# Inverse norms to row form: nine spreads on TensorE replaced by two transfers through DRAM each

## The chip, the cores and the metric

The kernel runs on one core of a Trainium2 chip. The metric is the device time of one execution in microseconds (us). Engines are named as in the profile: PE is TensorE, DVE is VectorE, ACT is ScalarE, POOL is GpSimd, SP is SyncE, which here only issues transfers.

## The reference, cut to what matters

A two-layer decoder trunk in f32: 512 tokens, model width 1024. Every layer is half a SwiGLU step, a token mixer, half a SwiGLU step and a gated embedding, each behind an RMS norm:

```python
def _rmsnorm(x, g):
    y = x32 * lax.rsqrt(jnp.mean(x32 * x32, axis=-1, keepdims=True) + EPS)
    return (y * g.astype(jnp.float32)).astype(x.dtype)
...
for li in range(DEPTH):                                  # DEPTH = 2
    x = x + 0.5 * _swiglu(_rmsnorm(x, g[0]), ...)
    h = _rmsnorm(x, g[1])
    x = x + (_hgrn2_mixer(h, ...) if li < N_A_LAYERS else _mla_mixer(h, ...))
    x = x + 0.5 * _swiglu(_rmsnorm(x, g[2]), ...)
    gate = jax.nn.sigmoid(_rmsnorm(x, g[3]) @ ple_w_gate[li])
    x = x + gate * (p[li] @ ple_w_in[li])
return _rmsnorm(x, final_norm)
```

The first layer's mixer is a gated linear recurrence with 8 heads of 128 (`_hgrn2_mixer`). Its output `o` is normed per head and token, with `_rmsnorm(o, out_gain)`, before an output gate and a projection. The second layer's mixer is latent attention.

## The kernel before

**Layout.** Activations stand transposed: model width on the 128 partitions, the 512 tokens along the free axis, so `x` is eight tiles of 128 x 512. A norm is not applied to the input of a product. The product is made with `gain * x`, and its result is multiplied by the inverse norm of each token, which must stand as a row, the same on every partition.

**Products.** Each f32 product is made of three matmuls on halves (`mm3`: hi*hi, hi*lo, lo*hi; lines 151 to 153, in the feed-forward parts L314). Weights come as tiles of 128 x 1024 in one long stream, `wall`. SP loads them (`raw`, five buffers), ACT cuts the high half (`whi`), DVE the low half (`wlo`, three buffers each; lines 129 and 130).

**The way of an inverse norm.** `Stats.add` sums squares over tiles. `column_sums` transposes the sum in four 128 x 128 pieces on PE (L214) and DVE sums each (L216), which gives four columns: token `j*128 + q` stands on partition `q` in column `j`. DVE scales and adds epsilon (L195), POOL raises to -0.5 (L198). `spread` turns the columns into a row on all partitions: four PE transposes of a broadcast column into a PSUM bank (L222). `rows` then copies the bank to the SBUF tile `rb` (ACT, L229). PSUM has four banks `mm` for products and four banks `aux` for the rest; `rb` tiles have two buffers.

**The recurrence** (`hgrn`, lines 628 to 905). Heads go in four pairs. `values` and `keys` make the products of a pair; `keys` multiplies by the stage's `rb`. `recur` is a generator for one head: dots of q and k (L205), masked to a diagonal on DVE (L708), three steps of scores on PE (L738) that DVE copies under a mask (L748) while it scales q (L724, L728, L753, L756) and POOL scales k (L760, L764), then larger scores (L782 to L801), the product with the values, its statistics, and the division by the norm (L829), which reads the spread from PSUM. `finish` multiplies by the gate `g`. The two heads of a pair alternate. `ple` is the gated embedding: eight products for `emb`, then eight with the gate, each multiplied by `rb` (L926); `last` is the same with the final norm.

**What sets the order.** In the recurrence up to the last pair and in the embeddings a scheduler places every instruction, by its own estimate of times and by priorities, in one fixed queue per engine; `soon` raises a priority. The feed-forward parts and PE's queue in the last pair (`FILL`) are written out by hand. Engines run their queue strictly in order, and an instruction that waits holds all behind it.

Of the kernel before, what the change touches and what calls it, by code (L numbers as in the profile page):

```python
# [9 lines left out]
F32 = mybir.dt.float32  # L10
# [3 lines left out]
ALU = mybir.AluOpType  # L14
AX = mybir.AxisListType

P = 128
T = 512
NT = T // P
# [38 lines left out]
def kernel(  # L58
# [11 lines left out]
    nc = tc.nc  # L70
    act, dve, pool, pe = nc.scalar, nc.vector, nc.gpsimd, nc.tensor
# [4 lines left out]
    tpool = ctx.enter_context(tc.tile_pool(name="tpool", bufs=1))  # L76
    qpool = ctx.enter_context(tc.tile_pool(name="qpool", bufs=1))
    psum = ctx.enter_context(tc.tile_pool(name="psum", bufs=1, space=bass.MemoryType.PSUM))

    count = [0]  # L80

    def name(s):
        count[0] += 1
        return f"{s}{count[0]}"

    def slot(s="s", dt=F32, tag="s"):
        return spool.tile([P, T], dt, tag=tag, bufs=BUFS[tag], name=name(s))
# [131 lines left out]
    def spread(r):  # L219
        pb = aux_bank()  # L220
        for j in range(NT):
            pe.transpose(pb[:, j * P : (j + 1) * P], r[:, j : j + 1].to_broadcast([P, P]), ident)  # L222
        return pb

    def rows(stats, sums=None):
        r = stats.columns(sums)
        pb = spread(r)
        rb = slot("rb", F32, "b")
        act.copy(rb, pb)  # L229
        return r, rb  # L230
# [395 lines left out]


    def hgrn(xg, stats, lower, upper, post):
        rt, rb = rows(stats)
        mk = slot("mk", I32)  # L630
        nc.scalar.dma_start(mk[:, 0 : 96 * len(STEPS)], msk)
        outs = [None] * A_HEADS
# [68 lines left out]
                decay += [t, new]  # L701
            return f, k, q, decay

        def recur(res, f, k, q, decay, v):
            dg = slot("D", F32, "r")
            pool.tensor_tensor(out=dg, in0=q, in1=k, op=ALU.mult)
            pd = column_dots(dg)
# [1 line left out]
                out=dg.rearrange("p (j q) -> p j q", j=NT),  # L709
                in0=ident.unsqueeze(1).to_broadcast([P, NT, P]),  # L710
                in1=pd.unsqueeze(2).to_broadcast([P, NT, P]),
                op=ALU.mult,
# [3 lines left out]
            q = qq[:, 0:T]  # L716
            yield
            for i, m in enumerate(STEPS):
# [6 lines left out]
                    out=qb[:, :, 1:3, :], in0=qa[:, :, 2:4, :],  # L725
                    in1=t[:, :, 1:3].unsqueeze(3).to_broadcast([P, nb, 2, m]), op=ALU.mult,
                )
                dve.tensor_tensor(  # L728
                    out=qb[:, :, 3, :], in0=qb[:, :, 2, :], in1=t[:, :, 1:2].to_broadcast([P, nb, m]), op=ALU.mult
# [4 lines left out]
                for half in range(2):  # L734
                    sc = aux_bank()
                    for e in range(2):
                        j = 2 * half + e
# [16 lines left out]
                    out=qa[:, :, 1, :], in0=qa[:, :, 1, :], in1=t[:, :, 0:1].to_broadcast([P, nb, m]), op=ALU.mult  # L754
                )
                dve.tensor_tensor(  # L756
                    out=qa[:, :, 2:4, :], in0=qb[:, :, 1:4:2, :],
                    in1=t[:, :, 0:1].unsqueeze(3).to_broadcast([P, nb, 2, m]), op=ALU.mult,
                )
                pool.tensor_tensor(  # L760
                    out=k4[:, :, 0:2, :], in0=k4[:, :, 0:2, :],
                    in1=u.unsqueeze(3).to_broadcast([P, nb, 2, m]), op=ALU.mult,
                )
                pool.tensor_tensor(  # L764
                    out=k4[:, :, 2, :], in0=k4[:, :, 2, :], in1=t[:, :, 3:4].to_broadcast([P, nb, m]), op=ALU.mult
# [38 lines left out]
            for j in range(NT):  # L804
                i, o = place[j]
# [12 lines left out]
            for j in range(NT):  # L818
                i, o = place[j]
# [6 lines left out]
            yield  # L826
            r = st.columns()
            yield
            dve.tensor_tensor(out=o1, in0=o1, in1=spread(r), op=ALU.mult)  # L829
            res.append(o1)  # L830

        def steps(rhs):
# [45 lines left out]
        done = None  # L878
        for p in range(pairs):
            res = [[], []]  # L880
            live = [recur(res[e], *fkq[e], vals[e]) for e in range(2)]
            if p == pairs - 1:
                break
            while live:
                live = [g for g in live if next(g, live) is not live]
            vals = values(p + 1)
            fkq = [keys(2 * p + 2 + e) for e in range(2)]
            if done is not None:
                for e in range(2):
                    finish(2 * p - 2 + e, *done[e], gate(2 * p - 2 + e))  # L890
            done = res
# [42 lines left out]
    def last(xg, pp, rb):  # L934
        scaled, stats, halves = [], Stats(KC - 1), []

        def post(m):
            stats.add(x[m])
            o = slot("xf")
            act.activation(o, x[m], AF.Copy, scale=gain(V_FIN, m))  # L940
            scaled.append(o)

        m = KC - 1
        emb = ple(xg, pp, rb, post, m)
        w = [block() for _ in range(KC)]
        half = T // 2
        for h in range(2):
            s = slice(h * half, (h + 1) * half)
            pg = mm_bank()
            for k in range(KC):  # L950
                mm3(pg[:, 0:half], w[k], tuple(a[:, s] for a in xg[k]), k == 0, k == KC - 1)
            g = slot("g", F32, "v")[:, 0:half]
            dve.tensor_tensor(out=g, in0=pg[:, 0:half], in1=rb[:, s], op=ALU.mult)
            act.activation(g, g, AF.Sigmoid)
            dve.tensor_tensor(out=g, in0=g, in1=emb[m][:, s], op=ALU.mult)
            dve.tensor_tensor(out=g, in0=x[m][:, s], in1=g, op=ALU.add)
            sq = slot("sq", F32, "r")[:, 0:half]
            act.activation(sq, g, AF.Square)
            sums = aux_bank()
            js = range(h * NT // 2, (h + 1) * NT // 2)  # L960
            for j in js:
                c = slice(j * P, (j + 1) * P)
                pe.matmul(sums[:, j : j + 1], stats.acc[:, c], ones, start=True, stop=False)
                pe.matmul(sums[:, j : j + 1], sq[:, c.start - s.start : c.stop - s.start], ones, start=False, stop=True)
            v, q = tiny(2), tiny(2)
            act.activation(v, sums[:, js[0] : js[-1] + 1], AF.Copy, scale=1.0 / D, bias=EPS)
            pool.tensor_tensor(out=q, in0=v, in1=mhalf[:, 0:2], op=ALU.pow)
            r = aux_bank()[:, 0:half]
            for n in range(2):
                pe.transpose(r[:, n * P : (n + 1) * P], q[:, n : n + 1].to_broadcast([P, P]), ident)  # L970
            halves.append((s, g, r))
        for s, g, r in halves:
            view = outT[:, s].rearrange("(i c p) t -> i p c t", c=2, p=P)
            for i in range(KC // 2):
                o = slot("o").rearrange("p (c t) -> p c t", c=2)
                for c in range(2):
                    n = 2 * i + c
                    if n == m:
                        dve.scalar_tensor_tensor(
                            out=o[:, c], in0=g, scalar=gain(V_FIN, m), in1=r, op0=ALU.mult, op1=ALU.mult  # L980
                        )
                    else:
                        dve.tensor_tensor(out=o[:, c], in0=scaled[n][:, s], in1=r, op=ALU.mult)
                nc.sync.dma_start(view[i], o)
# [309 lines left out]
    n3 = Next([gcol(0, 3)])  # L1294
    ffn(n2, n3, aside=embedding(0))
    n4 = Next([gcol(1, 0)])
    rb = rows(n3.stats)[1]
    sh = Shared()

    def both(m):  # L1300
# [12 lines left out]
    mla(n5.xg[0], n5.stats, cn, krope, sin, cos, n6)  # L1313
    n7 = Next([gcol(1, 3)])
    ffn(n6, n7, aside=embedding(1))
    last(n7.xg[0], held[1], rows(n7.stats)[1])


def _blocks(w):
# [166 lines left out]
```

## Time and profile before

| | us |
|---|---|
| median of 3 runs | 2166.73 (2166.57 to 2167.46) |
| the profiled execution | 2167.26 |
| its span, first to last instruction | 2165.5 |
| PE busy | 2143.4 |
| DVE busy | 1524.6 |
| ACT busy | 973.1 |
| POOL busy | 317.5 |

The feed-forward parts fill 0 to 360, 640 to 1010, 1100 to 1430 and 1750 to 2105 us, roughly; the recurrence runs from 360 to 650, the first embedding from 1010 to 1095, attention from 1430 to 1750, the last embedding from 2105 on. In the groups of instructions a row has line, engine, operation, output and inputs by the program's names, count, least, median and greatest duration in ns, and first and last start in us. In the timeline a row has start, duration, engine, line, operation and shapes, and in brackets how long the engine had stood and what ended it. In the chain of work that ended last a row has start, duration and the group. In the rows of transfers there are size and the median time from issue to landing. Matmul durations overlap, so what one costs is read from the distance of starts.

### The profile page before, as it was taken

The numbers are of one execution on the slowest core, as the hardware profiler recorded it, in microseconds if no ns is written. First come the engines' busy times: TensorE is split into PE (matmuls) and PEld (weight loads), VectorE is DVE, ScalarE is ACT, GpSimd is POOL, SyncE is SP. The second block draws the span as 40 slices with busy tenths as digits, with TensorE's granted clock in tenths as the row PEclk, the third lists the DMA queues.
The fourth block names the chain that finished last, engine by engine and source line by source line (L and its number), as shares of the span: only waits on it lengthen the run. The fifth ranks groups of instructions, "written<-read, shape, count | busy, mean of one in ns | idle before, by whom it ended". The sixth has DMA issues, their size and how long they took to land.

```text
span 2165.5 us, 32725 instructions
## 1 busy us (share of the span) xinstructions
PE 2143.4 (99%) x13026; PEld 1922.7 (89%) x13026; DVE 1524.6 (70%) x2261; ACT 973.1 (45%) x1374; POOL 317.5 (15%) x428
## 2 busy tenths in 40 slices
PE   8999999999999999999999999999999999999998
PEld 7899998889888899998888989988888888999987
DVE  6876675878786676676767757767676776775765
ACT  6354443323335353454553525446444563443544
POOL 2000001654521000001110000011110110000011
PEclk9999999999999999999999999999999999999999
DMA  5565553211223565552244656423122134655621
GB/s 193 151 166 156 142 160 100 72 67 60 68 69 104 149 173 149 146 156 98 94 120 133 163 152 161 134 100 96 61 82 90 50 107 130 156 163 127 186 98 49
DMA packets 76249, 261.46 MB, mean 121 GB/s; under 512 B 9152, under 2 KB 11328, under 8 KB 76096
## 3 DMA queue, kind: packets, MB, share of 16 engines
q1 hardware_dynamic: 64864, 220.15, 31.3%
q0 software_dynamic: 10368, 37.75, 10.3%
q8 instruction: 102, 1.67, 0.3%
q10 hardware_dynamic: 864, 1.46, 0.3%
q14 instruction: 51, 0.42, 0.1%
HBM read 253.04 MB, written 2.10 MB: 118 GB/s over the span
## 4 chain that ended last, share of the span: by engine, by line
PE 96%; DVE 2%; ACT 1%; issue 1%; DMA 0%; POOL 0%; DVEq 0%; SPq 0%; ACTq 0%
PE aux L314 19%; PE mm L151 18%; PE mm L152 18%; PE mm L153 18%; PE mm L314 14%; PE aux L152 1%; PE aux L153 1%; PE aux L738 1%; PE aux L151 1%; PE aux L1178 1%; PE aux L1152 0%; PE aux L1153 0%; PE aux L214 0%; ACT hi L166 0%; PE aux L222 0%
## 5 line engine op out<-in xcount | busy, mean ns | idle before, releaser
L151 PE MATMUL mm<-hi,whi 128*128 128x512 f32 x1656 | 647.4, 393 | 9.2 <-ACT whi L1267 5.7
L152 PE MATMUL mm<-lo,whi 128*128 128x512 f32 x1656 | 647.4, 391 | 0.6 <-DVE lo L167 0.6
L153 PE MATMUL mm<-hi,wlo 128*128 128x512 f32 x1656 | 646.4, 390 | 0.0
L305 DVE TENSOR_TENSOR wlo<-raw,whi 128x1024 fp32r<-128x1024 f32 x340 | 426.4, 1254 | 196.1 <-ACT whi L304 196.1
L304 ACT CAST whi<-raw 128x1024 fp32r<-128x1024 f32 x340 | 356.2, 1048 | 339.8 <-PE mm L152 177.1
L151 PEld LDWEIGHTS mm<-hi,whi 128*128 128x128 f32 x1656 | 311.3, 188 | 71.7 <-ACT whi L1267 5.7
L153 PEld LDWEIGHTS mm<-hi,wlo 128*128 128x128 f32 x1656 | 311.6, 188 | 63.6
L152 PEld LDWEIGHTS mm<-lo,whi 128*128 128x128 f32 x1656 | 311.9, 188 | 61.9 <-DVE lo L167 1.0
L314 PE MATMUL aux<-hi,whi 128*128 128x256 f32 x1152 | 326.0, 283 | 0.4 <-ACT mm L480 0.4
L314 PE MATMUL aux<-lo,whi 128*128 128x256 f32 x1152 | 326.1, 283 | 0.2 <-DVE lo L167 0.2
L314 PE MATMUL aux<-hi,wlo 128*128 128x256 f32 x1152 | 326.0, 283 | 0.0
L314 PE MATMUL mm<-hi,whi 128*128 128x256 f32 x864 | 244.5, 283 | 0.0
L314 PE MATMUL mm<-lo,whi 128*128 128x256 f32 x864 | 244.5, 283 | 0.0
L314 PE MATMUL mm<-hi,wlo 128*128 128x256 f32 x864 | 244.5, 283 | 0.0
L314 PEld LDWEIGHTS aux<-hi,whi 128*128 128x128 f32 x1152 | 221.1, 192 | 1.1 <-ACT mm L480 0.6
L314 PEld LDWEIGHTS aux<-lo,whi 128*128 128x128 f32 x1152 | 221.1, 192 | 0.9 <-DVE lo L167 0.4
L314 PEld LDWEIGHTS aux<-hi,wlo 128*128 128x128 f32 x1152 | 221.1, 192 | 0.0
L288 POOL DMA_DIRECT2D raw<-in_wall x72 | 62.7, 871 | 922.7 <-DMA raw<-in_wall 467.9
L129 ACT CAST whi<-raw 128x1024 fp32r<-128x1024 f32 x95 | 99.8, 1051 | 179.9 <-PE mm L152 122.5
L314 PEld LDWEIGHTS mm<-hi,whi 128*128 128x128 f32 x864 | 165.9, 192 | 0.0
L314 PEld LDWEIGHTS mm<-lo,whi 128*128 128x128 f32 x864 | 165.9, 192 | 0.0
L314 PEld LDWEIGHTS mm<-hi,wlo 128*128 128x128 f32 x864 | 165.9, 192 | 0.0
(250 smaller groups left out, 2888.2 us busy)
## 6 DMA issues: line engine op xcount, KB each, us to landing
raw<-in_wall SPq DMA_DIRECT2D x402, 512.0 KB, 3.5
raw<-in_wall POOLq DMA_DIRECT2D x72, 512.0 KB, 7.0
x<-in_xT SPq DMA_DIRECT2D x8, 256.0 KB, 5.9
qr<-hi SPq DMA_DIRECT2D x32, 64.0 KB, 2.0
qr<-lo SPq DMA_DIRECT2D x32, 64.0 KB, 2.0
out_dram<-o SPq DMA_DIRECT2D x8, 256.0 KB, 2.6
p<-in_pT ACTq DMA_DIRECT2D x4, 256.0 KB, 4.4
raw<-in_wall SPq DMA_DIRECT2D x2, 256.0 KB, 3.6
```

The lines of the kernel that those rows point to most:

```text
L129: act.copy(hi[:, s], raw[:, s])
L151: pe.matmul(out, a[0], b[0], start=first, stop=False)
L152: pe.matmul(out, a[0], b[1], start=False, stop=False)
L153: pe.matmul(out, a[1], b[0], start=False, stop=last)
L288: nc.gpsimd.dma_start(self.raw, wall[self.plus], accum_op=ALU.add)
L304: act.copy(hi, self.raw)
L305: dve.tensor_tensor(out=lo, in0=self.raw, in1=hi.bitcast(F32), op=ALU.subtract)
L314: pe.matmul(o, w[u][:, s], b[i][v], start=first and e + i + n == 0, stop=False, skip_group_check=True)
L738: pe.matmul(sc[:, e * 192 : (e + 1) * 192].rearrange("p (i b n) -> p i b n", i=2, n=3 * m), k[:, j * P : (j + 1) * P], q4[:, :, j * nbt : ...
L1178: pe.transpose(banks[b][:, o : o + P], prob[i][:, j * P : (j + 1) * P], ident)
```

## The change

At nine places the spread is replaced. `by_memory` writes the four columns to a line of 512 values in DRAM (128 partitions with four single values each, 512 values apart by 128) and reads the line back into `rb`, repeated on all 128 partitions. Both transfers are issued on SP, one waiting for the other. The places are the recurrence's own row (`rows` becomes `far_rows` in `hgrn`), the six heads of the first three pairs in `recur`, and the rows of both gated embeddings. The last pair keeps the spread (`near`), as do the feed-forward parts, the shared keys and attention.

```diff
+    dpool = ctx.enter_context(tc.tile_pool(name="dpool", bufs=1, space=bass.MemoryType.DRAM))
...
+    def by_memory(r):
+        line = dpool.tile([1, T], F32, tag="line", bufs=4, name=name("line"))
+        nc.sync.dma_start(line.rearrange("o (j q) -> (o q) j", j=NT), r)
+        rb = slot("rb", F32, "b")
+        nc.sync.dma_start(rb, line.to_broadcast([P, T]))
+        return rb
+
+    def far_rows(stats):
+        r = stats.columns()
+        return r, by_memory(r)
...
     def hgrn(xg, stats, lower, upper, post):
-        rt, rb = rows(stats)
+        rt, rb = far_rows(stats)
...
-        def recur(res, f, k, q, decay, v):
+        def recur(res, f, k, q, decay, v, near):
...
-            dve.tensor_tensor(out=o1, in0=o1, in1=spread(r), op=ALU.mult)
+            dve.tensor_tensor(out=o1, in0=o1, in1=spread(r) if near else by_memory(r), op=ALU.mult)
...
-            live = [recur(res[e], *fkq[e], vals[e]) for e in range(2)]
+            live = [recur(res[e], *fkq[e], vals[e], p == pairs - 1) for e in range(2)]
...
-    rb = rows(n3.stats)[1]
+    rb = far_rows(n3.stats)[1]
...
-    last(n7.xg[0], held[1], rows(n7.stats)[1])
+    last(n7.xg[0], held[1], far_rows(n7.stats)[1])
```

New lines shift the numbers: what stood at L151 to L222 now stands 2 lines further down, what stood from L229 on 13 lines. The scheduler places the first three pairs anew. Outside the recurrence the queues of PE, DVE, ACT and POOL are as before but for the instructions left out.

PE's queue at the end of the first pair, before. `aux_4084` is the second head's spread, `D_4376` and `D_4386` belong to the two heads of the second pair, `mm` are products of the next weights:

```order
L152 MATMUL mm_4766<-lo_3403,whi_4769 128x512
L153 MATMUL mm_4766<-hi_3402,wlo_4770 128x512
L222 MATMUL aux_4084<-cs,t_4068 128x128 x4
L205 MATMUL aux_4378<-ones,D_4376 128x1 x4
L205 MATMUL aux_4388<-ones,D_4386 128x1 x4
L738 MATMUL aux_4398<-qq_4384,k_4275 128x192 x2
L151 MATMUL mm_4711<-whi_4646,hi_3239 128x256
```

The same place now; `aux_4068` are the sums of the second head:

```order
L216 MATMUL aux_4068<-cs,sq_4052 128x128 x4
L155 MATMUL mm_4651<-whi_4641,lo_3323 128x256
L153 MATMUL mm_4651<-whi_4641,hi_3363 128x256
L207 MATMUL aux_4375<-ones,D_4373 128x1 x4
L154 MATMUL mm_4651<-wlo_4642,hi_3363 128x256
L155 MATMUL mm_4651<-whi_4641,lo_3364 128x256
L153 MATMUL mm_4651<-whi_4647,hi_3404 128x256
L207 MATMUL aux_4385<-ones,D_4383 128x1 x4
L751 MATMUL aux_4395<-qq_4381,k_4272 128x192 x2
```

The second pair's dots and scores no longer stand behind the spreads; they follow the sums, and the 128x512 products that stood between have moved behind the scores.

DVE's queue at that place, before. `o` are the outputs of the first pair:

```order
L650 SCALAR_TENSOR_TENSOR vlo_4713<-mm_4711,t_3529,vhi_4712 128x256
L829 TENSOR_TENSOR o_4035<-o_4035,aux_4078 128x512
L829 TENSOR_TENSOR o_4052<-o_4052,aux_4084 128x512
L708 TENSOR_TENSOR D_4376<-cs,aux_4378 128x512
L708 TENSOR_TENSOR D_4386<-cs,aux_4388 128x512
L748 COPY_PREDICATED D_4376<-mk_3546,aux_4398 128x64x3
L748 COPY_PREDICATED D_4376<-mk_3546,aux_4398 128x64x2
```

And now:

```order
L721 TENSOR_TENSOR D_4373<-cs,aux_4375 128x512
L721 TENSOR_TENSOR D_4383<-cs,aux_4385 128x512
L761 COPY_PREDICATED D_4373<-mk_3545,aux_4395 128x64x3
L761 COPY_PREDICATED D_4373<-mk_3545,aux_4395 128x64x2
L842 TENSOR_TENSOR o_4034<-o_4034,rb_4079 128x512
L761 COPY_PREDICATED D_4373<-mk_3545,aux_4395 128x64
L761 COPY_PREDICATED D_4373<-mk_3545,aux_4401 128x64x3
```

The product with the row (L829, now L842) has moved into the second pair's first step, between the masked copies of its first scores; what stands behind it there waits for it.

PE's queue at the end of the third pair, before; `aux_5255` are sums, `aux_5264` and `aux_5270` the spreads, `D_5710` is of the last pair:

```order
L214 MATMUL aux_5255<-cs,sq_5239 128x128 x4
L152 MATMUL mm_5674<-lo_3483,whi_5677 128x512
L153 MATMUL mm_5674<-hi_3482,wlo_5678 128x512
L151 MATMUL mm_5674<-hi_3520,whi_5677 128x512
L152 MATMUL mm_5674<-lo_3521,whi_5677 128x512
L153 MATMUL mm_5674<-hi_3520,wlo_5678 128x512
L222 MATMUL aux_5264<-cs,t_5243 128x128 x4
L222 MATMUL aux_5270<-cs,t_5254 128x128 x4
L205 MATMUL aux_5712<-ones,D_5710 128x1 x4
```

And now, at the start of the last pair:

```order
L155 MATMUL mm_5667<-hi_3484,wlo_5671 128x512
L153 MATMUL mm_5667<-hi_3522,whi_5670 128x512
L154 MATMUL mm_5667<-lo_3523,whi_5670 128x512
L155 MATMUL mm_5667<-hi_3522,wlo_5671 128x512
L207 MATMUL aux_5705<-ones,D_5703 128x1 x4
L153 MATMUL mm_5723<-hi_3241,whi_5726 128x512
```

The sums of the third pair have moved up; between them and the first dots of the last pair stand 80 product matmuls and no spread.

## The prediction

> **What bounds the kernel now.** I read the busy totals first, then the chain of work that ended last, then the engines by stretch.
>
> ```profile
> PE 2143.4 (99%) x13026; PEld 1922.7 (89%) x13026; DVE 1524.6 (70%) x2261; ACT 973.1 (45%) x1374; POOL 317.5 (15%) x428
> PE 96%; DVE 2%; ACT 1%; issue 1%; DMA 0%; POOL 0%; DVEq 0%; SPq 0%; ACTq 0%
> 444.00:460.00 16.00, 16.00 (x120) 15.26 (x119) 8.98 (x16) 2.26 (x5) 6.62 (x10) 1.00 0.01 2
> ```
>
> TensorE (PE) is busy for 99% of the span and is 96% of the chain. The last row is the end of the first pair of heads and the start of the second (columns: sum, PE, PEld, DVE, ACT, POOL, granted clock, DMA share, GB/s): PE never stands, VectorE (DVE) works 9.0 of the 16 us from 444, and the DMA engines do nothing. So work taken from PE is worth its full time, as long as no new wait reaches PE; all that goes to DMA is free until someone waits for it.
>
> **What the change takes from PE.** Nine spreads of four transposes go. The price of one is read where it stands among plain matmuls:
>
> ```profile
> L222 PE MATMUL aux<-cs,t x68: 270/272/323, 30.6 to 2113.2; 128*128 128x128 f32 x68
> 449.82 0.28 PE L152 MATMUL mm<-wlo,hi 128*128 128x256 f32 x1
> 449.94 0.28 PE L153 MATMUL mm<-whi,lo 128*128 128x256 f32 x1
> 450.30 0.40 PE L152 MATMUL mm<-lo,whi 128*128 128x512 f32 x1
> 450.53 0.60 PE L222 MATMUL aux<-cs,t 128*128 128x128 f32 x4
> 450.89 0.48 PE L153 MATMUL mm<-hi,wlo 128*128 128x512 f32 x1
> 451.20 0.39 PE L151 MATMUL mm<-hi,whi 128*128 128x512 f32 x1
> 450.69 0.44 PE aux L222 x4
> ```
>
> Each transpose lasts 272 ns, but they overlap: from the start of the spread (450.53) to the second matmul behind it (451.20) are 0.67 us, of which one 512-column matmul is the usual 0.23 (450.30 to 450.53); 0.44 is left, and the chain (last row) books the same. (A 256-column matmul takes 0.12, from 449.82 to 449.94.) So 9 x 0.44 = 4.0 us leave PE. 68 transposes are 17 spreads; 8 stay.
>
> The Trainium skill ("TensorE: Matmul & The Clock Gate", Part 4: PE-mode transpose) gives about 275 ns for a transpose within a kernel. The 272 ns row agrees for a single one, the 0.44 for four does not make it a price per piece; what it would give is the last rival below.
>
> At the third pair the spread also waits:
>
> ```profile
> 581.12 0.65 PE L222 MATMUL aux<-cs,t 128*128 128x128 f32 x4 [0.48 <-POOL t L198]
> PE aux L222 <- POOL t L198: 0.5, 1, 0.5
> ```
>
> PE stands 0.5 us there for the power on POOL. After the change no PE instruction at that place needs the power, and 80 ordinary matmuls stand behind the sums: I book -0.5.
>
> ```profile
> L229 ACT COPY rb<-aux x5: 583/588/588, 31.2 to 2113.5; 128x512 f32<-128x512 f32 x5
> ```
>
> ScalarE loses three of these copies to rb (0.59 us each), and DVE reads the rows from SBUF instead of PSUM. ACT is 45% busy and not in the chain; I book nothing for either. If ACT were late, its cover would be the weight halves, which it cuts ahead of PE.
>
> **What it adds: two transfers in a row.** No row shows a scatter of 512 four-byte pieces to DRAM. Nearest rows:
>
> ```profile
> vc<-in_vec SPq DMA_DIRECT2D x1, 51.5 KB, 1.8
> qr<-hi SPq DMA_DIRECT2D x32, 64.0 KB, 2.0
> pos<-in_pos ACTq DMA_DIRECT2D x1, 256.0 KB, 3.5
> raw<-in_wall SPq DMA_DIRECT2D x402, 512.0 KB, 3.5
> q10 hardware_dynamic: 864, 1.46, 0.3%
> ```
>
> The write moves 2 KB: 1.8 us from below. Its 512 pieces are the doubt: queue 10's 864 packets (1.46 MB, 1.7 KB each) took 0.3% of 16 engines' span, 104 us or 120 ns each; 32 pieces an engine would make 3.9 us at that price, so 5.7 from above. I take 2.0, as for qr, which is nearest in size and is also written by SP; the 120 ns are for pieces 400 times larger, partly amid other traffic. The read is 128 copies of one 2 KB line, which is exactly what pos is: 3.5 us from above, in a stage where DMA is busier; 2.0 from below; I take 2.5, as these engines stand idle (0.01 above). The round trip c is then 4.5 us, between 3.8 and 9.2. Eighteen small issues on SP (0.33 us each) hide: SP issues no load between these two rows, which are neighbours in its queue, and the four new transfers of the first pair fall between them.
>
> ```profile
> 438.24 0.33 SPq L120 DMA_DIRECT2D raw<-in_wall  x1
> 464.72 0.33 SPq L120 DMA_DIRECT2D raw<-in_wall  x1
> ```
>
> SP does stand in these transfers (the read waits for the write, the second read for DVE's first product, since one of two rb buffers is held by the stage's own row), and the loads of the next weights queue behind. At the later pairs it is the same; a load of 3.5 us lies five buffers ahead of its use, so some us of SP cost nothing. POOL's queue gets nothing new.
>
> **Where rb is waited for.** Three single places first, power and first use:
>
> ```profile
> 364.37 1.04 POOL L198 TENSOR_TENSOR t<-t,mhalf 128x4 f32<-128x4 f32 x1 [10.34 <-DVE t L195]
> 369.06 0.69 DVE L668 TENSOR_TENSOR f<-mm,rb 128x512 f32<-128x512 f32 x1
> 1012.89 1.04 POOL L198 TENSOR_TENSOR t<-t,mhalf 128x4 f32<-128x4 f32 x1 [10.88 <-DVE t L195]
> 1020.67 0.69 DVE L926 TENSOR_TENSOR g<-mm,rb 128x512 f32<-128x512 f32 x1 [3.85 <-PE mm L153]
> 2107.40 1.04 POOL L198 TENSOR_TENSOR t<-t,mhalf 128x4 f32<-128x4 f32 x1 [10.89 <-DVE t L195]
> 2115.18 0.69 DVE L926 TENSOR_TENSOR g<-mm,rb 128x512 f32<-128x512 f32 x1 [3.86 <-PE mm L153]
> ```
>
> Power's end to first use: 3.7, 6.7 and 6.7 us. Both embeddings hold 4.5, and at 9.2 DVE would stand 2.5 us with two tiles of weights cut. At the recurrence's start DVE stands about 0.8 us (5.5 at worst). Behind it in its queue are an eviction and a weight half that PE needs a tile (24 matmuls of 0.23, 5.5 us) later; PE has four mm banks and goes on. Zero for all three; 1 us at the worst c, if the banks ran out.
>
> The pairs are the question. At the first pair:
>
> ```profile
> 447.40 0.44 PE aux L214 x4
> 447.46 1.02 POOL L198 TENSOR_TENSOR t<-t,mhalf 128x4 f32<-128x4 f32 x1
> 454.56 1.68 PE aux L205 x16
> 457.84 0.65 PE aux L738 x4
> 457.04 1.93 DVE L748 COPY_PREDICATED D<-mk,aux 128x192 f32<-128x192 int32 x4
> 458.83 0.82 DVE L753 TENSOR_TENSOR qq<-qq,f 128x128 f32<-128x128 f32 x1
> 461.91 0.41 DVE L728 TENSOR_TENSOR qq<-qq,T 128x128 f32<-128x128 f32 x1
> 462.85 0.38 DVE L753 TENSOR_TENSOR qq<-qq,f 128x128 f32<-128x128 f32 x1
> 467.28 0.56 DVE L728 TENSOR_TENSOR qq<-qq,T 128x128 f32<-128x128 f32 x1
> 458.63 0.74 POOL L760 TENSOR_TENSOR k<-k,T 128x256 f32<-128x256 f32 x1 [8.77 <-PE aux L738]
> L748 DVE COPY_PREDICATED D<-mk,aux x144: 216/361/587, 398.3 to 607.8; 128x192 f32<-128x192 int32 x48, 128x128 f32<-128x128 int32 x48, 128x64 f32<-128x64 int32 x48
> ```
>
> Everything here is 0.4 earlier, by the spread that is gone at 365. The power of the first head ends at 448.48 - 0.44 = 448.0; its row lands at 448.0 + c = 452.5. In the new order PE goes from the sums (end 447.4) straight to the second pair: two small matmuls (0.24), dots (0.84), three (0.36), dots (0.84), scores (0.65), so 450.3. DVE does two masked copies of these scores (0.59 + 0.36) and is at the product at 451.3: it stands c - 3.3 = 1.2 us (0.5 to 5.9). Does PE feel it? Before, DVE went from 457.04 to 462.3 (5.2 us) for the first head's step; 0.95 of it is done, 4.3 stay, with 0.7 for the product: ready at 456.3 plus the stand. PE asks for it after 2 dots (1.68), 4 score rows (2.6), 20 matmuls of 0.12 and 21 of 0.23, 11.5 us behind 447.4, at 458.9: 2.6 us to spare. For the second head PE asks 2.1 us later (461.0). DVE took from 462.3 to 467.8 for it, with two weight halves and an eviction between that the new order mostly puts later; 3.5 with the product is my estimate (459.8 plus the stand): 1.2 to spare, and by the next step about 1. So of DVE's stand, 1.1 us is free. By the count PE stands c - 4.4 = 0.1 us, at worst 4.8, at best 0; I take 0.4, since three hand-overs with 1 us of room stand in a row and an instruction of DVE's took 0.82 while POOL worked (458.83) and 0.38 while it didn't (462.85).
>
> At the second pair 14 DVE instructions lie between the power's input and the product, against 6 here, some 6 us, so about c - 6.5 reaches PE: +0.2 for what the count leaves out (0 to 2.7). At the third the matmuls behind (80 x 0.23 = 18 us) cover all: 0.
>
> **The sum.** -4.0 - 0.5 + 0.4 + 0.2 = -3.9 us. Against the profiled execution (2167.26, span 2165.5 and 1.8 around it) that is 2163.4; it stood 0.53 above the median of the three runs, so against the median of 2166.73 it is 2162.8. About 0.2%, or 4.3 us, is what a measurement can tell from no change: the forecast lies just inside.
>
> **Rivals.**
> - No wait reaches PE: -4.5, 2162.2, just past the bound. For it: 1.1 us of room and a stand of 1.2. Against: three hand-overs in a row.
> - The write is slow: at its upper price of 5.7, c = 8.2, PE stands 3.8 at the first pair and 1.7 at the second, -4.5 + 5.5 = +1.0: 2167.7. For it: 512 pieces of 4 bytes, which no row shows. The Trainium skill ("DMA: Bandwidth & Descriptors", Specifications) says that pieces under 512 B are not written at line rate but read, changed and written; no run here shows it yet.
> - Slower than before: the round trip is far longer, and DVE's stand in front of the product becomes PE's at both pairs. PE stands c - 4.4 at the first and about c - 6.5 at the second; the gain of 4.5 is eaten at c = 7.7, and at 9.9 the kernel is 0.2% slower; at c = 12 it would be 13.1 - 4.5 = 8.6 us slower, 2175.3. For it: loads here took up to 8.2 us (below). Against: those are loads of 512 KB in busy stages.
> - The transposes cost their 272 ns each: 36 x 0.272 = 9.8, -9.7 in all, 2157.0. Against: four take 0.60 us as one piece.
>
> ```profile
> DMA to landing us min/median/max: 3.0/3.5/8.2
> ```
>
> **How the numbers follow.** Forecast 0.40, no wait 0.28, slow write 0.16, slower 0.11, transposes at full price 0.03, other effects of the new order 0.02. Faster by over 0.2% (under 2162.4): no wait 0.27, the full price 0.03, the forecast's lower edge 0.10: 0.40. Slower: 0.11. Within: 0.49. The range takes in the first three cases, with 0.6 us below the no-wait time for waits on DVE in the last pair that may shrink: 2161.6 to 2167.8.
>
> **What would show it.** Right: PE busy about 3.9 us less; no wait of L222 for POOL but at the start; both transfers landing 4 to 5 us after the power; a DVE stand of about 1 us before the product of the first pair; PE without idle between 450 and 470. Wrong: an idle PE in front of scores there, with DVE as releaser and DMA behind it; a line transfer over 3 us; weight casts that wait for DMA.

## The result: 39 us slower

The changed kernel takes 2205.75 us (median of 4 runs, 2203.57 to 2207.09) against 2166.65 for the kernel before (4 runs, 2166.28 to 2167.46): a ratio of 1.0180 (95% interval 1.0168 to 1.0192). The forecast was 2162.8, with a range up to 2167.8. The profiled execution took 2205.72 us with a span of 2203.9, 38.4 more than the 2165.5 of before.

The profile page after: busy totals, and the chain of work that ended last, by engine.

```profile
PE 2154.7 (98%) x12990; PEld 1930.1 (88%) x12990; DVE 1518.5 (69%) x2261; ACT 971.5 (44%) x1371; POOL 316.1 (14%) x428
PE 88%; DMA 4%; DVE 3%; issue 2%; ACT 2%; POOL 1%; SPq 0%; POOLq 0%; DVEq 0%; ACTq 0%
```

36 transposes are gone, and yet PE is busy for 11 us more; DMA, which was 0% of the chain, is 4%. The two transfers, first the write (L229), then the read (L231), with those who waited for the read (us, times):

```profile
DMA to landing us min/median/max: 7.6/8.4/11.8
...
  DVE o L842: 38.9, 6
  DVE g L939: 22.1, 2
  DVE f L681: 10.1, 1
...
DMA to landing us min/median/max: 3.0/4.1/5.5
```

VectorE stood at all nine places, 71 us in all. At the first pair, VectorE's timeline and then TensorE's (idle time and its releaser in brackets):

```profile
454.85 0.45 DVE L761 COPY_PREDICATED D<-mk,aux 128x128 f32<-128x128 int32 x1
465.66 0.69 DVE L842 TENSOR_TENSOR o<-o,rb 128x512 f32<-128x512 f32 x1 [10.37 <-DMA rb<-line]
...
468.04 0.40 DVE L737 TENSOR_TENSOR qq<-qq,T 128x256 f32<-128x256 f32 x1
...
469.24 0.28 DVE L741 TENSOR_TENSOR qq<-qq,T 128x128 f32<-128x128 f32 x1
...
474.68 0.69 DVE L842 TENSOR_TENSOR o<-o,rb 128x512 f32<-128x512 f32 x1 [5.15 <-DMA rb<-line]
```

```profile
462.45 0.39 PE L155 MATMUL mm<-hi,wlo 128*128 128x512 f32 x1
469.67 2.90 PE L751 MATMUL aux<-qq,k 128*128 128x192 f32 x8 [6.83 <-DVE qq L741]
472.11 0.88 PE L153 MATMUL mm<-hi,whi 128*128 128x512 f32 x1
476.93 0.58 PE L153 MATMUL mm<-whi,hi 128*128 128x256 f32 x1 [3.94 <-DVE vlo L663]
```

The write was issued at 451.98 and the row landed at 465.64, 13.7 us later. VectorE stands 10.37 us in front of the product; the scaling of q for the next scores is behind it; PE stands 6.83 us in front of these scores. Its other 3.94 us are for the low half of a piece of the values (`vlo`), which VectorE makes behind the second head's product, and that product stood 5.15 us for the second head's row. The second head's power, and the two writes in the chain of work that ended last:

```profile
452.32 1.02 POOL L200 TENSOR_TENSOR t<-t,mhalf 128x4 f32<-128x4 f32 x1 [0.36 <-DVE t L197]
...
451.98 10.32 DMA line<-t
462.69 7.61 DMA line<-t
```

SP's queue holds the first head's read, which waits for the first write, ahead of the second head's write. So the second write started at 462.69, 9.4 us after the power that it carries, and the second row landed at 474.65, 21.3 us after that power. At the third pair the second row came 18.8 us after its power; at the second pair, where both writes went out ahead of the reads, 15.3.

At the third pair, VectorE and then TensorE:

```profile
609.45 0.69 DVE L842 TENSOR_TENSOR o<-o,rb 128x512 f32<-128x512 f32 x1 [7.41 <-DMA rb<-line]
610.06 0.68 DVE L871 TENSOR_TENSOR g<-mm,rb 128x512 f32<-128x512 f32 x1
610.66 1.21 DVE L132 TENSOR_TENSOR wlo<-raw,whi 128x1024 fp32r<-128x1024 f32 x1
```

```profile
606.32 0.40 PE L154 MATMUL mm<-lo,whi 128*128 128x512 f32 x1
611.93 0.80 PE L155 MATMUL mm<-hi,wlo 128*128 128x512 f32 x1 [5.22 <-DVE wlo L132]
```

Behind the waiting product stood the low half of the next weights, and PE ran out of them. The second cost is in the column of the granted clock (the columns are: stretch, sum, PE, PEld, DVE, ACT, POOL, granted clock, DMA share, GB/s):

```profile
381.58:384.99 3.41, 3.41 (x10) 2.64 (x9) 3.41 (x4) 0.00 (x0) 3.31 (x2) 0.50 0.83 241
466.92:480.57 13.65, 6.97 (x23) 6.38 (x23) 8.46 (x32) 0.00 (x0) 1.05 (x2) 0.50 0.12 20
538.60:545.43 6.83, 4.76 (x18) 4.79 (x19) 6.47 (x21) 0.00 (x0) 1.14 (x2) 0.50 0.11 38
610.28:620.52 10.24, 8.59 (x27) 7.63 (x27) 9.52 (x14) 4.39 (x6) 0.00 (x0) 0.50 0.36 130
1067.66:1071.07 3.41, 3.41 (x10) 2.66 (x9) 2.59 (x4) 1.58 (x3) 0.00 (x0) 0.50 0.40 141
```

The same stages before:

```profile
360.00:440.00 80.00, 80.00 (x472) 71.09 (x472) 55.32 (x113) 25.06 (x38) 37.07 (x64) 1.00 0.24 79
500.00:530.00 30.00, 30.00 (x210) 28.28 (x209) 22.68 (x46) 9.74 (x16) 10.14 (x13) 1.00 0.08 22
1000.00:1100.00 100.00, 100.00 (x450) 82.77 (x449) 66.06 (x84) 55.72 (x80) 15.07 (x14) 1.00 0.30 96
```

Behind every one of these stands the clock is at half for a multiple of 3.41 us; before, it was at 1.0 in all these stages. At half the clock, half of the time that PE is busy there counts as lost. The account of the 38.4 us, in us (stands read from the timeline of PE, clock from the rows above):

| place | forecast of PE's stand | stand | lost by the clock |
|---|---|---|---|
| recurrence's start | 0 (1 at worst) | 2.5 | 1.7 |
| first pair | 0.4 (0 to 4.8) | 10.8 | 3.5 |
| second pair | 0.2 (0 to 2.7) | 6.6 | 2.4 |
| third pair | 0 | 5.2 | 4.3 |
| first embedding | 0 | 2.4 | 1.7 |
| last embedding and end | 0 | 1.0 | 0.7 |
| sum | 0.6 | 28.5 | 14.3 |

28.5 + 14.3 - 4.5 (nine spreads and the wait for POOL) = 38.3.

### The profile page after: what moved, and what is told of

It reads as the page before. It is cut to its first block, busy times and chain, and to the rows that moved or that the text cites. A ratio compares the mean times of both kernels' runs of the same rounds, so it can differ in the third digit from the quotient of the medians.

```text
span 2203.9 us, 32669 instructions
## 1 busy us (share of the span) xinstructions
PE 2154.7 (98%) x12990; PEld 1930.1 (88%) x12990; DVE 1518.5 (69%) x2261; ACT 971.5 (44%) x1371; POOL 316.1 (14%) x428
## 4 chain that ended last, share of the span: by engine, by line
PE 88%; DMA 4%; DVE 3%; issue 2%; ACT 2%; POOL 1%; SPq 0%; POOLq 0%; DVEq 0%; ACTq 0%
PE aux L327 19%; PE mm L153 16%; PE mm L155 16%; PE mm L154 16%; PE mm L327 14%; DMA line<-t 3%; PE aux L154 1%; PE aux L155 1%; PE aux L153 1%; PE aux L751 1%; DMA rb<-line 1%; DVE wlo L132 1%; PE aux L1191 1%; PE aux L1165 0%; PE aux L1166 0%
```

## The experiments

Theory A: the round trip through memory is about 13 us instead of 4.5; VectorE waits for it in the middle of its queue, what stands behind the product stops PE, and the clock does the rest. The rivals are named as the runs test them.

**The transfers without the wait.** All nine round trips beside the spreads, which stay in use:

```diff
+    def shadow(r):
+        line = dpool.tile([1, T], F32, tag="line", bufs=4, name=name("line"))
+        nc.sync.dma_start(line.rearrange("o (j q) -> (o q) j", j=NT), r)
+        dead = tpool.tile([P, P], F32, tag="dead", bufs=1, name=name("dead"))
+        nc.sync.dma_start(dead, line[:, 0:P].to_broadcast([P, P]))
```

> The kernel before, every engine's queue as before, with the nine round trips added on SP alone: the columns are written as 512 single values to the line and its first 128 values are read back on 128 partitions (64 KB instead of 256, for want of space) into a tile that nobody reads; the spreads on TensorE stay and are used. Theory A (the round trip is long, and only those who wait for the row lose): the writes land after 8 to 12 us as in the changed kernel, no PE stand appears at the nine places, the granted clock stays 1.0 until the end, and the time is 2166.7 within 1.5 us. Rival B (the transfers hurt by themselves, because SP stands in them and the next weights load late, or because 512 pieces crowd the loads): most of the 39 us are here too, 2185 to 2205, with weight casts that wait for DMA at the six pair places.

Measured: 2166.61 us against 2166.39, ratio 1.0001 (0.9992 to 1.0010). The landing times of the write, and the three pairs' places by engine:

```profile
DMA to landing us min/median/max: 8.3/9.2/11.6
```

```profile
444.00:470.00 26.00, 26.00 (x170) 24.05 (x169) 19.54 (x41) 5.12 (x8) 10.17 (x11) 1.00 0.04 4
506.00:532.00 26.00, 26.00 (x175) 24.22 (x174) 18.69 (x40) 5.75 (x9) 7.68 (x9) 1.00 0.11 5
574.00:602.00 28.00, 27.08 (x144) 23.34 (x143) 23.69 (x58) 6.14 (x8) 9.05 (x12) 1.00 0.20 34
```

The writes are as slow as in the changed kernel, and the time doesn't move: PE is busy throughout but for the 0.9 us that it also stood before, the clock is 1.0. SP standing in the transfers and the crowding of DMA cost the weight loads nothing, as the prediction had it. Rival B is out: the loss is made by those who wait for the row, or by the new order of the pairs.

**The two halves of the change.** Only the three rows of the stages through memory, the heads spread again; then the reverse:

```diff
-            dve.tensor_tensor(out=o1, in0=o1, in1=spread(r) if near else by_memory(r), op=ALU.mult)
+            dve.tensor_tensor(out=o1, in0=o1, in1=spread(r), op=ALU.mult)
```

```diff
-        rt, rb = far_rows(stats)
+        rt, rb = rows(stats)
...
-    rb = far_rows(n3.stats)[1]
+    rb = rows(n3.stats)[1]
...
-    last(n7.xg[0], held[1], far_rows(n7.stats)[1])
+    last(n7.xg[0], held[1], rows(n7.stats)[1])
```

> The changed kernel with the spread put back at the six heads; the rows of the recurrence and of both embeddings still go through memory. My forecast of the change was 0 us of waiting here, and 3 x 0.44 saved: 2165.3. Theory A, by the stands and half-clock windows of the changed kernel's trace at these places (4.2 us at the recurrence's start, 4.25 in the first embedding, 1.1 in the last): 2176, between 2172 and 2179. Rival C (the new order of the first three pairs costs the time, not the round trip): this order is the old one, so 2166 or less.

> The other half: the six heads go through memory, the three rows are spread on TensorE as before. Theory A: the rest of the loss, 39.1 - 9.5 = 30 us: 2196, between 2190 and 2201, with PE stands behind DVE's product with the row and windows of half the granted clock at all three pairs. If the loss of the pairs hangs on the stand at the recurrence's start (two rb buffers, one held late by the stage's own row), it would fall to 10 us or less here: 2177 or less.

Measured: the rows alone 2176.56 us (ratio 1.0047, 1.0033 to 1.0061), the heads alone 2198.64 (1.0149, 1.0135 to 1.0163). 10.2 and 32.3 over before; together 42 where the whole has 39, so they add up but for about 3 us, for which the runs show no single place. Theory A's numbers were 2176 and 2196. The rows, which the prediction had at no waiting at all, cost a quarter of the loss. The second run has PE's and VectorE's queues in the pairs as in the changed kernel, and no stand at the start: the stands in the pairs don't hang on it.

**The same transfers, the product later.** The row is needed only when the head's output meets its gate, a pair later. The rows of the stages are spread.

```diff
-            dve.tensor_tensor(out=o1, in0=o1, in1=spread(r) if near else by_memory(r), op=ALU.mult)
-            res.append(o1)
+            if near:
+                dve.tensor_tensor(out=o1, in0=o1, in1=spread(r), op=ALU.mult)
+                res.append((o1, None))
+            else:
+                res.append((o1, by_memory(r)))
...
-        def finish(h, o1, sg):
+        def finish(h, o1, row, sg):
+            if row is not None:
+                dve.tensor_tensor(out=sg, in0=row, in1=sg, op=ALU.mult)
...
-        rb = slot("rb", F32, "b")
+        rb = slot("rb", F32, "s")
```

> The six heads through memory, but the product with the row is moved from the end of a head to where the head's gate is applied, a pair later: the gate is multiplied by the row there (one VectorE product of 128x512 in either case), and the row has a tile of its own kind, not one of the two rb buffers. The three rows are spread as before. Theory A (it is the waiting product in VectorE's queue that costs the time): the row lands after 10 to 14 us, some 40 us before its use, no PE stand is left, the clock stays 1.0 and the six spreads and the wait for the power are saved: 2166.7 - 6 x 0.44 - 0.5 = 2163.6, between 2162 and 2166. Rival B or C (transfers themselves, or the new order of the pairs, which is again another one): PE stands at the pair places stay, 2180 or more.

Measured: 2178.28 us, ratio 1.0055 (1.0042 to 1.0067). A miss for theory A's 2163.6. Nobody waited for a row any more, but PE waited for something else (us in total, times, longest):

```profile
PE mm L153 <- DVE f L681: 6.1, 3, 2.6
```

f is the keys' product with the stage's row, long there. In VectorE's queue the next pair's f and q now stood behind the sums of the pair that ends:

```
425 L218 TENSOR_REDUCE t_4076<-aux_4071 128x4
426 L197 TENSOR_SCALAR t_4069<-t_4076 128x4
427 L681 TENSOR_TENSOR f_4272<-mm_4210,rb_3546 128x512
428 L682 SCALAR_TENSOR_TENSOR q_4274<-mm_4241,rb_3546 128x512
```

My reason (rival D): the row was the only new thing in the pool of 40 buffers from which f comes too, and a pool hands its buffers out in turn; f got one that was still held. The next run gives the row a buffer of the head outputs instead, and changes nothing else.

```diff
-        rb = slot("rb", F32, "s")
+        rb = slot("rb", F32, "p")
```

> As the kernel with the late product, but the row's tile comes from the pool of the head outputs (o1) instead of the general one of 40 buffers. In the run before, the three pairs' sums stood ahead of the next keys' first product f on VectorE, and TensorE waited 6.1 us in 3 pieces for f. Rival D (the general pool hands its buffers out in turn, so a row that waits for its head's end takes the buffer that f would have had, and f comes after it): here f stands where it stood in the kernel before, no TensorE wait for f of over 1 us is left, and with the row landing before its use the time is 2166.4 - 2.6 - 0.5 = 2163.3, between 2162 and 2166. Rival C (any new order of the pairs costs some 10 us; the late product as such): again 2175 or more. What both leave open: the third pair's rows are used only some 15 us after the power; if they come later, a stand there.

Measured: 2163.56 us against 2166.88, ratio 0.9985 (0.9976 to 0.9994). f stands where it stood before, PE's wait for it is gone, and the six spreads and the wait for POOL are saved: 3.3 us, 3.1 by the prediction's prices. The round trip is no shorter here (writes land 9.5 to 14.2 us after issue). At the third pair rows still come after VectorE asks for them, which the expectation had left open; VectorE's and PE's waits there:

```profile
DVE g L880 <- DMA rb<-line: 4.3, 2, 3.9
PE aux L751 <- DVE qq L741: 1.2, 1, 1.2
```

The 1.2 us were 0.4 before. So theory A holds, and rival C (a new order of the pairs costs as such) falls for this order; the run before shows that another order can cost some 12 us by accident. Rival D's remedy works, since the pool is the only edit; that the buffers' turn is the reason is my reading of the queue. That the changed kernel's own order costs nothing by itself is argued from its trace, where each new stand follows a wait for the row, and was not run.

**A shorter round trip.** The line in the order (q, j): a partition's four values lie side by side, 128 pieces of 16 bytes; VectorE reads the row through a permuted view.

```diff
-        nc.sync.dma_start(line.rearrange("o (j q) -> (o q) j", j=NT), r)
+        nc.sync.dma_start(line.rearrange("o (q j) -> (o q) j", j=NT), r)
...
-        return rb
+        return rb.rearrange("p (q j) -> p j q", j=NT)
```

> The changed kernel with the line in another order: a partition's four values stand side by side, so the write has 128 pieces of 16 bytes instead of 512 of 4, and VectorE reads the row through a permuted view at all nine places. The scheduler places the product a few instructions earlier. Theory A with a price per piece (the write takes about 2.0 us and 12.5 ns for each of its pieces, from 8.4 us for 512): the write lands after 3.6 us, the round trip is 7 us instead of 12.5, VectorE's stands shrink by 5.5 us each; the embeddings (6.7 us of cover) stand no more, at the first pair some 3 us of stand are left, and the time is 2167, between 2163 and 2173. Rival E (what costs is a small write to DRAM as such, whatever the count): the write stays at 8 us and the time at 2200 or more. Against A would also be a VectorE product that the permuted view makes slow (0.7 us as now, or over 1).

Measured: 2170.37 us, ratio 1.0016 (1.0007 to 1.0025): 35 us of the loss gone with the rearranged write and the order of the pairs that the scheduler made with it. At the start and in the embeddings, where the order is as in the changed kernel, the write alone did it: PE's stands of 2.5 and 2.4 us are gone. The landing times of the write, then who waited for the read:

```profile
DMA to landing us min/median/max: 1.4/2.5/3.2
```

```profile
  DVE o L845: 10.6, 5
  DVE g L942: 7.4, 2
  ACT whi L131: 4.7, 1
  DVE f L684: 3.2, 1
```

VectorE's stands at the pairs fall from 38.9 us to 10.6, PE's to 5.7 in four pieces of 0.8 to 2.2, and the clock stays at 1.0 up to the end. The permuted view is not free: the product takes 1.13 us (median) instead of 0.69.

**What makes the write slow.** First, two unused writes of different shape at each place:

```diff
+        if i == 0:
+            nc.sync.dma_start(line[:, 0:P].rearrange("o (j q) -> (o q) j", j=1), r[:, 0:1])
+        elif i == 1:
+            nc.sync.dma_start(line[:, 0 : 2 * P].rearrange("o (j q) -> (o q) j", j=2), r[:, 0:2])
+        elif i == 2:
+            nc.sync.dma_start(line.rearrange("o (j q) -> (o q) j", j=NT), r)
+        elif i == 3:
+            nc.sync.dma_start(line.rearrange("o (q j) -> (o q) j", j=NT), r)
+        elif i == 4:
+            nc.sync.dma_start(line.rearrange("o (j q) -> (o j) q", j=NT), cs[0:NT, 0:P])
+        else:
+            nc.sync.dma_start(dead, r[:, 0:1])
```

> The kernel before with two unused writes at each of the nine places, one waiting for the other, six shapes in turn, three of each: 128, 256 and 512 single values of 4 bytes to DRAM, 128 pieces of 16 bytes to DRAM, four pieces of 512 bytes to DRAM, and 128 single values into one partition of SBUF. Only the landing times count. Price per piece: 3.6, 5.2, 8.4, 3.6, 2.0 and 3.6 us. Rival E (DRAM must read, change and write for pieces under 512 bytes, and that is what takes the time, not the count): all small writes to DRAM near 8, four pieces of 512 bytes and the write to SBUF near 2.

Inconclusive: the second was issued 0.4 us after the first, in spite of what I had meant, and both landed together (8.3 to 15.1 us). Only the last, 128 values into one partition of SBUF, was alone: 1.94 us. So, in two more kernels, one at a time, the spacing w being 16 values at first and then 1 to 16:

```diff
+            nc.sync.dma_start(line.rearrange("o (j q w) -> (o q) j w", j=NT, w=w)[:, :, 0], v[:, 0:NT])
```

> The kernel before with fourteen unused writes, one at a place and at least 9 us apart, each engine's queue but SP's as before: from a tile with values of the place, (a) 128 single values side by side, (b) 256, (c) 512, all in the layout of the changed kernel; (g) 512 single values 64 bytes apart and (h) 128 such; (f) 128 single values into one partition of SBUF. In the run before, two writes went together at each place and hid each other. Price per single value, the same for all (16 ns each from 8.3 us for 512 in the last embedding): a, h and f 2.1, b 4.1, c and g 8.3. Rival E1 (neighbouring 4-byte values from different engines fall into one line of DRAM and wait for one another): g and h are fast, near 2, while a is slower than f. Rival E2 (a fixed price of a small write to DRAM): excluded already by 128 pieces of 16 bytes, 1.4 us.

> The kernel before with fourteen unused writes of all four columns, one at a place, only their spacing differs: 512 single values 4, 8, 16, 32 and 64 bytes apart, and 128 pieces of 16 bytes side by side. The run before had 8.5 us for 4 bytes apart and 1.8 for 64. Rival E1 (values that fall into one line of DRAM wait for one another, about 1 us each): the time falls with the number of values in a line. For a line of 64 bytes some 8, 8, 4 to 5, 2.5 and 1.8 us; for one of 32 bytes 8, 4 to 5, 2.5, 1.8 and 1.8; for one of 16 bytes 8, 4, 1.8, 1.8, 1.8. The pieces of 16 bytes stay at 1.4 to 3, by whatever line. Rival E3 (only the step of 4 bytes is slow, because the transfer is taken for one of contiguous values): 8 us at 4 bytes and 1.8 at all others.

Measured, us from issue to landing, each single transfer (the kernels took 2167.58 and 2166.14 us, one run each, as before):

| write | landing |
|---|---|
| 512 values, 4 bytes apart | 8.5, 9.6, 11.8 |
| 256 values, 4 bytes apart | 9.3, 9.5, 10.3 |
| 128 values, 4 bytes apart | 7.2, 7.6, 9.2 |
| 512 values, 8 bytes apart | 3.7, 4.2, 5.4 |
| 512 values, 16 bytes apart | 2.9, 2.9, 4.9 |
| 512 values, 32 bytes apart | 1.9, 2.2, 2.7 |
| 512 values, 64 bytes apart | 1.8, 1.8, 1.8, 2.7 |
| 128 values, 64 bytes apart | 1.4, 3.0 |
| 128 pieces of 16 bytes, side by side | 1.4, 3.2 |
| 128 values to one partition of SBUF | 1.9, 1.9 |

The price per piece, by which the expectations had reckoned since the 16-byte pieces, is wrong: 512 values 64 bytes apart land in 1.8 to 2.7 us, 128 packed ones need 7.2 to 9.2. That the 16-byte pieces landed within its 3.6 us was luck. What counts is how close together small values fall in DRAM, as E1 had it: the time falls steadily with the spacing and is nearly flat from about 32 bytes on, so the rival with the step of 4 bytes alone (E3) is out too. 128 packed values into SBUF take 1.9 us, so it hangs on DRAM. The Trainium skill ("DMA: Bandwidth & Descriptors", Specifications), which the prediction cited, says that pieces under 512 bytes are read, changed and written. All the pieces here are shorter, and most of the writes are fast: by these runs shortness alone doesn't make a write slow. That close values wait for one another, and in which unit, wasn't measured.

**When the clock falls.** The kernel before with one stand of PE in each group of the feed-forward parts:

```diff
+    def stand(ps, ops):
+        t, u = slot("st", F32, "r"), slot("su", F32, "r")
+        pe.transpose(ps[:, 0:P], ident, ident)
+        act.copy(t[:, 0:P], ps[:, 0:P])
+        pool.tensor_tensor(out=t[:, 0:P], in0=t[:, 0:P], in1=t[:, 0:P], op=ALU.mult)
+        for n in ops:
+            pool.tensor_tensor(out=u[:, 0:n], in0=cs[:, 0:n], in1=cs[:, 0:n], op=ALU.mult)
+        pool.tensor_tensor(out=t[:, 0:P], in0=t[:, 0:P], in1=t[:, 0:P], op=ALU.mult)
+        pe.transpose(ps[:, 0:P], t[:, 0:P], ident)
...
                 ps, k = mm_bank(), 0
+                if m == 3:
+                    stand(ps, STANDS[stand_n[0]])
```

> The kernel before, with one stand of TensorE put into each of the twelve groups of the feed-forward parts: a transpose, its copy by ScalarE, two to eight products on GpSimd and a transpose that waits for them; nothing of it is used. The stands grow from about 2.5 us to about 11. To be seen: from which stand on the granted clock falls, and for how long. Theory F (the clock follows TensorE's recent load, as the windows behind the stands of the changed kernel suggest: one of 3.41 us behind 2 to 3 us, four behind 4.6 us and a group of small waits): no fall below 2 us, one half-clock window of 3.41 us behind 2.5 to 4 us, two or more behind the longer ones, 1.7 us lost in each. Rival G (the clock falls only where waits come one after another, as in the pairs): a single stand of under 5 us leaves the clock at 1.0.

Measured: 2247.6 us (one run); the twelve stands were 2.0 to 8.4 us long, 56.5 in all. Each group here is a window of 3.41 us with what follows it (columns as above):

```profile
85.06:88.47 3.41, 1.45 (x8) 1.00 0.14 26
88.47:91.88 3.41, 3.41 (x10) 0.50 0.94 231
...
334.23:337.64 3.41, 2.52 (x12) 1.81 (x10) 2.46 (x3) 0.91 (x2) 1.63 (x3) 1.00 0.06 10
337.64:341.05 3.41, 2.08 (x10) 1.74 (x11) 1.92 (x3) 2.18 (x3) 2.61 (x3) 1.00 0.41 149
341.05:344.46 3.41, 3.41 (x17) 2.83 (x16) 0.81 (x1) 0.00 (x0) 0.00 (x0) 1.00 0.44 144
...
2139.89:2143.30 3.41, 0.00 (x0) 0.00 (x0) 1.89 (x4) 2.20 (x4) 3.23 (x3) 1.00 0.48 154
2143.30:2153.54 10.24, 5.52 (x14) 4.37 (x15) 1.18 (x1) 0.00 (x0) 5.66 (x6) 0.50 0.17 53
```

In the first two rows, where PE and not the others are listed, a stand of 1.96 us lies whole in one window, and the next runs at half clock: it holds 10 matmuls, against 17 in the last of the next three rows. In those three, a stand of 2.2 us is cut by a window's edge into 0.9 and 1.3, and the clock stays. All windows at half clock begin on one grid of 3.41 us. Rival G is out, and theory F has the size but not the rule: it's not the length of a stand that decides but how much of it falls into one window of the grid. Over the twelve stands, and those of the changed kernel, of its two halves and of the late product, all 24 windows at full clock with 1.85 us or more of standing were followed by half clock, and none with up to 1.79. Left out are the first 10 us or so, for which the traces have no clock, and the last stage with its many tiny matmuls, where half clock came behind windows with 1.1 to 2.2 us of standing. How long half clock lasts isn't settled: at the start of the recurrence in the changed kernel one window without a stand ended it, at its third pair it took two. The Trainium skill ("TensorE: Matmul & The Clock Gate", Part 1: The HAM clock gate) tells of a free-running window of 3413 ns and of half the clock after an idle one. The grid agrees; by these runs the window needn't be idle, a little over half of it was enough.

**The best of it.** Late product, 16-byte pieces, all nine places through memory:

```diff
 # against the late product with the row in the pool of the head outputs
-        nc.sync.dma_start(line.rearrange("o (j q) -> (o q) j", j=NT), r)
+        nc.sync.dma_start(line.rearrange("o (q j) -> (o q) j", j=NT), r)
...
-                dve.tensor_tensor(out=sg, in0=row, in1=sg, op=ALU.mult)
+                dve.tensor_tensor(out=tj(sg), in0=row, in1=tj(sg), op=ALU.mult)
...
-        rt, rb = rows(stats)
+        rt, rb = far_rows(stats)
...
-    rb = rows(n3.stats)[1]
+    rb = far_rows(n3.stats)[1]
...
-    last(n7.xg[0], held[1], rows(n7.stats)[1])
+    last(n7.xg[0], held[1], far_rows(n7.stats)[1])
```

> The late product with the row in a tile of the head outputs, now with the write in 128 pieces of 16 bytes and with all nine places through memory; PE's and VectorE's queues are those of the kernel with the late product but for the three spreads that are gone. The product with the row reads a permuted view and takes 1.1 us instead of 0.69, beside TensorE. Theory A: no TensorE stand at any of the nine places, so 9 x 0.44 + 0.5 = 4.5 us less than before: 2162.2, between 2161 and 2164.5; 0.3 to 1.3 less than the late product alone. If VectorE stands in front of the recurrence's first f (3 us in the run with the wide pieces) reach TensorE, or the slower products do, up to 2166.

Measured: 2162.33 us against 2166.82, ratio 0.9980 (0.9971 to 0.9989). 4.5 us are saved, which is nine times 0.44 and the 0.5 of POOL. VectorE still waits twice for a row, 5.7 us in all. At the nine places PE has no stand of over 0.7 us; the longest is at the third pair, where it was 0.4 before:

```profile
PE aux L754 <- DVE qq L744: 0.7, 1, 0.7
```

It beats both kernels. Against the late product alone (0.9985) it can't be told apart.

## Why the prediction was wrong

- **The spreads, -4.0, and POOL's wait, -0.5: right.** Where no wait takes their place, the runs save 3.3 us in the pairs, for which 3.1 were booked, and 4.5 at all nine places, for which 4.5 were, each within 2 us either way. That leaves nothing for ScalarE's copies and VectorE's source, as booked.
- **The line's write, 2.0 us (1.8 to 5.7): this is the step that failed.** It measured 8.4 (7.6 to 11.8), beyond even the upper end. The prediction priced 512 pieces by a row with packets 400 times larger; what is slow is 4-byte values that lie side by side in DRAM (512 of them 64 bytes apart land in 1.8 us), which no row of before had. The doubt was named, but its upper bound was taken from a row that couldn't hold it. The read, 2.5 (2.0 to 3.5), measured 4.1 (3.0 to 5.5). The round trip was 13 to 14 us for the first row of each pair instead of 4.5.
- **SP and DMA, 0: right for the weights, wrong for the second row of a pair.** The round trips without the wait cost the loads nothing. But the prediction named SP's order and put no time on it: at the first and third pair the second write stood behind the first read, its row landed 21.3 and 18.8 us after its power, and PE's 3.94 us at the first pair and 5.22 at the third follow from these second rows.
- **VectorE's stand, c - 3.3, and PE's at the first two pairs, c - 4.4 and c - 6.5: the mechanism was right.** With the measured c of 13.7, VectorE should stand 10.4 and did 10.37; PE should stand 9.3 in front of the scores and did 6.83, and that the 3.94 of the second row bring it near again, to 10.8, is luck. At the second pair c was 13.1, so about 6.6, and PE stood 6.62.
- **The third pair, 0: wrong.** The 80 matmuls were there, but a matmul needs its weights, and their low halves are cut by VectorE behind the waiting product. PE stood 5.2 us. The prediction counted PE's queue and not VectorE's.
- **The recurrence's start and the embeddings, 0 (1 at worst): wrong by c.** VectorE stood 10 to 11 us, PE 2.5 and 2.4, and 1.0 more at the end.
- **What a stand costs: missing.** The sum took a stand of PE as its own length. The clock took another 14.3 us, more than a third of the loss. The Trainium skill's page named above ("TensorE: Matmul & The Clock Gate", Part 1: The HAM clock gate) has half the clock behind an idle window. The prediction, whose range had stands of up to 4.8 us, put no price on the clock.
- **The rivals.** The slower one had the place, the mechanism and the turning point (c = 7.7), and said what would show it; with c at 13.7 and 13.1 its own sum gives -4.5 + 9.3 + 6.6, 11 us slower. The chance of 0.11 was too small, since nothing in the profile excluded such a c, and its size lacked the second rows, the third pair, the single rows and the clock.

## What to carry to other kernels

When values go through DRAM to change their layout, price the write by how its pieces lie in memory, not by bytes or count: four values side by side per partition made the round trip half as long. Where two round trips share a queue, issue both writes ahead of the first read: at the second pair, where it came so, the second row landed 3.8 us behind the first, at the other two 9 and 12. Put the consumer of a slow transfer where nothing urgent stands behind it in its engine's queue, and give the transferred tile a pool whose turn doesn't hold up others; then even round trips of 14 us and more cost next to nothing. And count a stand of TensorE at its length plus 1.7 us or more of half clock once over 1.8 us of it can fall into one window of 3.41 us: here stands of 2.2 and 3.2 us cut by a window's edge cost no and one window of half clock.

## What was not expected of the hardware

- 128 values of 4 bytes, written side by side to DRAM from 128 partitions, take 7.2 to 9.2 us; 512 of them 64 bytes apart 1.8 to 2.7.
- The granted clock is decided on a fixed grid of 3.41 us: outside the last stage, 1.85 us of standing in one window halved it for the next, 1.79 didn't.
- A VectorE product whose one source is read with a step of four values took 1.13 us (median of six) for 128x512 instead of 0.69.
